# Expert weights of a mixture-of-experts stage fetched one expert per transfer, in runs of 8 KB

## The chip, the cores and the metric

The kernel runs on 1 core of one Trainium2 chip. The metric is the device time of one execution in microseconds (us); lower is better. The time before is 997.18 us, the median of 3 runs (996.82 to 998.98). Below, TensorE is PE, VectorE DVE, ScalarE ACT, GpSimd POOL, and SyncE, which issues the loads, SP.

## What is computed

One decoder block on 528 tokens (16 meta tokens and 512 real ones) of width 1024, in float32: two token mixers, then a mixture of experts, then a norm. The change touches the experts alone. Each token goes to 2 of 32 experts. An expert is two matrices of 1024 x 512 and one of 512 x 1024:

```
y = (silu(xb @ w_gate[e]) * (xb @ w_up[e])) @ w_down[e]
out = zeros.at[slot_tok].add(y * weight)
```

## The kernel before

The token mixers fill the first half of the time. Their weights, too, come in through SP (tiles `raw`), and between these SP already issues the first expert weights. Then the router picks experts (lines 885 to 960), and the loop `for p in range(last_p + 1)` runs over 16 pairs of experts. Each expert has room for 64 tokens, so a pair fills the 128 partitions of a result: expert 0 of the pair (`e` = 0) makes the partitions 0 to 63, expert 1 the others. In each pair:

- `ahead` (matmuls `pw`, line 976) finds the tokens of the next pair, and POOL gathers their rows from DRAM into `XG` (line 983);
- `up_proj` makes the gate product `pgt` and the up product `put` (line 1014): 8 steps over `k`, in each one matmul of expert 0 and one of expert 1;
- `glu` joins them on ACT and DVE into `HG`; `hidden_T` transposes it (`pht`); `operand` transposes the next pair's tokens (`pxs`, line 1006);
- `down_proj` (`py`, line 1033) has 4 steps over `k` for each of two halves of the columns, again with both experts in each;
- `combine` (`pcb`, line 1047) adds the previous pair's result to the tokens, 16 matmuls a pair.

Matmuls of the experts are float32 and fill half of the array's columns ("128*64" in the profile), those of `pcb`, `pw`, `pht` and `pxs` the whole array ("128*128"). The trace has two records for each float32 matmul instruction, one for `pcb` and the transposes. So the 16 instructions of one `put` are 32 records.

The weights of a pair come in 12 transfers of 1 MB, 4 for each of `w_gate`, `w_up` and `w_down`. `CUTS` says how they are cut. `fetch` (line 759) issues a transfer and notes in `at` which tile holds which part; `prefetch` issues as many as there are free buffers ("slots"); `take` hands a pair's tiles to the matmuls, `weight` picks one matmul's part, and `feed` gives the slots back after a product. Two places are cut otherwise and stay so: part of the first pair's gate (`pieces0`) and the last pair's `w_down`, in transfers of 512 KB. A loop behind the main one (line 1206) takes experts with more than 64 tokens; it is not entered with these inputs.

The order of `pgt`, `put`, `py`, `pw` and `pcb` on PE is not that of the text. A scheduler fixes each engine's order when the program is built, by its own estimate of when operands are there, so that a matmul whose weights it expects late goes behind others.

Of the kernel before, what the change touches and what calls it, by code (L numbers as in the profile page):

```python
# [8 lines left out]
F32 = mybir.dt.float32  # L9
# [29 lines left out]
def hybrid_block_kernel(ctx: ExitStack, tc: tile.TileContext, x, meta, norm1_g, w_in, hg_lb,  # L39
# [4 lines left out]
    PE, ACT, DVE, POOL, SP = nc.tensor, nc.scalar, nc.vector, nc.gpsimd, nc.sync  # L44
# [21 lines left out]
    def uniq(name):  # L66
        seq[0] += 1
        return f"{name}_{seq[0]}"

    def slot(shape, dtype, name):  # L70
        s = free.pop(0)
        return pool_of[s].tile(shape, dtype, name=uniq(name), tag=s), s

    def give(*ss):
        free.extend(ss)

    def ms(tag, shape, dtype, name):
        return misc.tile(shape, dtype, name=uniq(name), tag="m" + tag)

    def ps(shape, name, dtype=F32):  # L80
        return psum.tile(shape, dtype, name=name, tag="ps")

    def bc_row(ap1d, n):
        return bass.AP(tensor=ap1d.tensor, offset=ap1d.offset, ap=[[0, 128], [1, n]])
# [158 lines left out]
    for i in range(2):  # L243
        a, s = slot([128, 4, N], F32R, "hnH")
        b, s2 = slot([128, 4, N], F32R, "hnL")
# [13 lines left out]
    for i in range(5):  # L259
        t_ = tmp.tile([128, D], F32, name="xt", bufs=5)  # L260
# [72 lines left out]
    p = ps([128, 512], "pc")  # L333
# [74 lines left out]
    oaH, s = slot([128, 4, T], F32R, "oaH")  # L408
# [320 lines left out]
    for i in range(2):  # L729
        t_, s = slot([128, 2, D], F32, "h")  # L730
# [3 lines left out]
    def tk(lst, t, a=0, b=D):  # L734
        return lst[t // 2][:, t % 2, a:b]
# [2 lines left out]

    EW = [(w[0].rearrange("e (p k) c -> p e k c", p=128), nk) for w, nk in ((w_gate, 8), (w_up, 8), (w_down, 4))]
    last_p = NE // 2 - 1
    CUTS = [[(k, k + 2, 0, 512) for k in range(0, 8, 2)]] * 2 + [[(k, k + 1, 0, 1024) for k in range(4)]]
    pieces, pieces0 = [], []
    for p_ in range(last_p + 1):
        for m in range(3):
            cuts = CUTS[m]
            if p_ == 0 and m == 0:
                cuts = cuts[:2]
                pieces0 = [(0, 0, k, k + 1, 0, 512) for k in range(4, 8)]  # L750
            if p_ == last_p and m == 2:
                cuts = [(k, k + 1, c, c + 512) for c in (0, 512) for k in range(4)]
            pieces += [(m, p_) + c for c in cuts]
    at = {}
    nxt = [0]

    def fetch(t_, s, piece):
        m, p, k0, k1, c0, c1 = piece
        SP.dma_start(t_, EW[m][0][:, 2 * p:2 * p + 2, k0:k1, c0:c1])
        for k in range(k0, k1):  # L760
            at.setdefault((m, p), {})[k, c0 // 512] = (t_[:, :, k - k0], c0, s)

    def prefetch(n=len(pieces)):
        while n and nxt[0] < len(pieces) and free:
            n -= 1
            piece = pieces[nxt[0]]
            nxt[0] += 1
            t_, s = slot([128, 2, piece[3] - piece[2], piece[5] - piece[4]], F32, "wx")
            fetch(t_, s, piece)

    def weight(tab, e, k, c0):

        t_, b, _ = tab.get((k, c0 // 512)) or tab[k, 0]
        return t_[:, e, c0 - b:c0 - b + 512]

    def take(m, p):
        tab = at.pop((m, p))
        return tab, sorted({s for _, _, s in tab.values() if s})

    def gate(dst):  # L780
        got = []
# [213 lines left out]
    def token_onehots(i, sw):  # L995
        oht = OHT[:, i]
        DVE.tensor_scalar(oht, iotat, sw[:, 2:3], None, op0=OP.is_equal)
        return oht

    def operand():  # L1000

        xv = XG.rearrange("s (p k) -> s k p", k=8)
        for q in range(2):
            p_ = ps([128, 4, 128], "pxs")
            for k in range(4):
                PE.transpose(p_[:, k], xv[:, 4 * q + k], ident)  # L1006
            DVE.tensor_tensor(XS[:, 4 * q:4 * q + 4], p_,
                              g2k[:, 4 * q:4 * q + 4][:, :, None].to_broadcast([128, 4, 128]), op=OP.mult)

    def up_proj(w2, name):  # L1010
        p_ = ps([128, FE], name)
        for k in range(8):
            for e in range(2):
                PE.matmul(p_[CAP * e:CAP * e + CAP], XS[:, k, CAP * e:CAP * e + CAP],  # L1014
                          weight(w2, e, k, 0), start=(k == 0), stop=(k == 7))
        return p_

    def glu(pg, pu, sw):
        ACT.activation(HG, pg, AF.Silu, scale=sw[:, 1:2])  # L1019
        DVE.scalar_tensor_tensor(HG, pu, sw[:, 1:2], HG, op0=OP.mult, op1=OP.mult)  # L1020

    def hidden_T():

        pt = ps([128, 4, 128], "pht")
        hv = HG.rearrange("s (p k) -> s k p", k=4)
        for k in range(4):
            PE.transpose(pt[:, k], hv[:, k], ident)  # L1027
        ACT.activation(HT, pt.rearrange("p f s -> p (f s)"), AF.Copy)  # L1028
# [7 lines left out]
    def down_proj(w2, half, sw):  # L1036
        p_ = ps([128, 512], "py")
        down_steps(p_, w2, half, range(4))
        yh = Y[half][:, 0]
        ACT.activation(yh, p_, AF.Copy, scale=sw[:, 0:1])  # L1040
        DVE.scalar_tensor_tensor(Y[half][:, 1], p_, sw[:, 0:1], yh.bitcast(F32), op0=OP.mult, op1=OP.subtract)  # L1041

    def combine(oht, half):
        for t in range(4):
            p_ = ps([128, 512], "pcb")
            for i in range(2):
                PE.matmul(p_, oht[:, 128 * t:128 * t + 128], Y[half][:, i],  # L1047
                          start=(i == 0), stop=(i == 1))
            hs = tk(h32, t, 512 * half, 512 * half + 512)
            DVE.tensor_add(hs, hs, p_)  # L1050

    def ahead(p):

        onehots(OH, RK[:, :, 2 * p:2 * p + 2])
        pw = by_slot(OH, TAB[:, :, p])
        gather(pw[:, 3:4])
        return slot_weights(pw)
# [109 lines left out]


    wd, ss_ = take(2, last_p)
    u0, s = slot([128, 4, 512], F32, "u0")  # L1170
    sq, s2 = slot([128, 512], F32, "sqf")
# [29 lines left out]
    with tc.If(nr > 0):  # L1201
        XG = ms("A", [128, D], F32, "XG")
        POOL.memset(XG, 0.0)
        DVE.tensor_scalar(RK, RK, float(-CAP), None, op0=OP.add)
        with tc.For_i(0, nr):
            with tc.For_i(0, NE // 4) as i4:

                for i in range(2):
                    sw = ahead(i)
                    oht = token_onehots(i, sw)  # L1210
                    operand()
                    tabs, ss = [], []
                    for (w, nk), cuts in zip(EW, CUTS):
                        tabs.append({})
                        for k0, k1, _, c1 in cuts:
                            t_, s = slot([128, 2, k1 - k0, c1], F32, "wx")
                            SP.dma_start(t_, w[:, bass.ds(i4 * 4 + 2 * i, 2), k0:k1, :])
                            ss.append(s)
                            for k in range(k0, k1):
                                tabs[-1][k, 0] = (t_[:, :, k - k0], 0, s)  # L1220
                    glu(up_proj(tabs[0], "pgt"), up_proj(tabs[1], "put"), sw)
                    hidden_T()
                    for half in range(2):
                        down_proj(tabs[2], half, sw)
                        combine(oht, half)
                    give(*ss)
                rk2 = HG[:, :4 * NE].rearrange("p (t e) -> p t e", t=4)
                tab2 = HT[:, :8 * NE].rearrange("p (t e c) -> p t e c", t=4, c=4)
                DVE.tensor_copy(rk2[:, :, :NE - 4], RK[:, :, 4:])
                DVE.tensor_scalar(rk2[:, :, NE - 4:], RK[:, :, :4], float(-CAP), None, op0=OP.add)  # L1230
                DVE.tensor_copy(RK, rk2)
                DVE.tensor_copy(tab2[:, :, :NE // 2 - 2], TAB[:, :, 2:])
                DVE.tensor_copy(tab2[:, :, NE // 2 - 2:], TAB[:, :, :2])
                DVE.tensor_copy(TAB, tab2)

        gfb = ms("A", [128, D], F32, "gfb")
        SP.dma_start(gfb, bc_row(final_g, D))
        for t in range(4):
            sq, s = slot([128, D], F32, "sqf")
            o, s2 = slot([128, D], F32, "o")  # L1240
            ACT.activation(sq, tk(h32, t), AF.Square, accum_out=SS[:, 0, t:t + 1])
            rs = SS[:, 2, t:t + 1]
            rms_scale(rs, SS[:, 0, t:t + 1], D)
            DVE.scalar_tensor_tensor(o, tk(h32, t), rs, gfb, op0=OP.mult, op1=OP.mult)
            SP.dma_start(out2[128 * t:128 * t + 128], o)
            give(s, s2)
# [29 lines left out]
```

## Time and profile before

| what | value |
|---|---|
| median of 3 runs | 997.18 us (996.82 to 998.98) |
| the profiled execution: time, span | 998.75 us, 997.0 us |
| PE busy | 936.4 us (94%) |
| PE weight loads busy | 602.8 us (60%) |
| DVE, ACT, POOL busy | 448.3, 255.9, 246.0 us |
| read from DRAM, written | 250.89 MB, 4.19 MB |
| mean granted clock of PE | 0.974 |

The span runs from the first to the last instruction of the profiled execution, and times in the trace count from its start. Busy time of PE counts a matmul from its start to its modelled end, so a pipelined stream shows as fully busy. The profile's second part cuts the span into 40 slices of 24.9 us; PEclk there is the clock granted to PE in tenths of 2.4 GHz (9 stands for 90% or more), DMA the mean busy share of the core's 16 DMA engines, GB/s what they moved. In the timeline a row is a run of like instructions: start, length, engine, line, operation, result and operands, number of records.

### The profile page before, as it was taken

To read this page: it belongs to the slowest core of one execution; us is meant where nothing else is said; L and a number is where in the kernel's file an instruction comes from. 1 tells how busy PE (TensorE), PEld (TensorE's weight loads), DVE (VectorE), ACT (ScalarE), POOL (GpSimd) and SP (SyncE) were. 2 spreads that over 40 slices of the span, in tenths; PEclk is the share of its full clock that TensorE was granted. 3 is DMA by queue.
4 is the path that set the end of the run, shared out by engine and by line. 5 is a ranking of instruction groups with operands and counts; after the bars stand their busy time and mean duration, and the time that the engine had idled before them with its cause. 6 is when DMAs were issued, how large, how long until landed. Compare 5 with 4: busy or idle time off the path is not lost.

```text
span 997.0 us, 12289 instructions
## 1 busy us (share of the span) xinstructions
PE 936.4 (94%) x4812; PEld 602.8 (60%) x4812; DVE 448.3 (45%) x931; ACT 255.9 (26%) x456; POOL 246.0 (25%) x167
## 2 busy tenths in 40 slices
PE   7989999989979999999859999999999999999984
PEld 5979998879868888888733444443334343433331
DVE  5678448786772323232532443333334333333323
ACT  6445536876750000000401110100110100010004
POOL 4542443254465454545200000000000000000002
PEclk9999999999988999999959999999999999999998
DMA  6221112212563223238969999999999999999992
GB/s 215 77 92 45 44 53 85 62 45 85 218 236 100 96 91 99 92 99 312 389 258 328 409 407 408 408 409 408 409 409 409 408 408 408 408 408 409 409 356 87
DMA packets 94298, 251.76 MB, mean 253 GB/s; under 512 B 6582, under 2 KB 39434, under 8 KB 94235
## 3 DMA queue, kind: packets, MB, share of 16 engines
q1 hardware_dynamic: 91352, 244.61, 64.4%
q0 software_dynamic: 2304, 4.20, 1.2%
q10 hardware_dynamic: 578, 2.10, 0.5%
q8 instruction: 40, 0.66, 0.3%
q14 instruction: 24, 0.19, 0.1%
HBM read 250.89 MB, written 4.19 MB: 256 GB/s over the span
## 4 chain that ended last, share of the span: by engine, by line
PE 80%; DVE 7%; DMA 5%; ACT 4%; POOL 2%; issue 2%; SPq 0%; POOLq 0%; DVEq 0%; ACTq 0%
PE pj L204 27%; PE put L1014 11%; PE pgt L1014 10%; PE py L1033 10%; PE pcb L1047 7%; DMA wx<-in_w_up_dram 4%; PE po L799 3%; PE pl L545 2%; PE pw L976 2%; PE pxs L1006 1%; PE po L1071 1%; PE pj L311 1%; PE pht L1027 1%; POOL hl L91 1%; DMA XG<-HD,idx 1%
## 5 line engine op out<-in xcount | busy, mean ns | idle before, releaser
L204 PE MATMUL pj<-hnH,hl 128*128 128x512 f32 (+1 forms) x960 | 252.9, 353 | 9.5 <-POOL hl L91 7.2
L91 POOL TENSOR_TENSOR hl<-raw,hl 128x1024 fp32r<-128x1024 f32 (+1 forms) x76 | 174.9, 2303 | 202.2 <-ACT hl L88 100.0
L204 PEld LDWEIGHTS pj<-hnH,hl 128*128 128x128 f32 x960 | 163.9, 192 | 33.5 <-POOL hl L91 8.5
L204 PE MATMUL pj<-hnL,hl 128*128 128x512 f32 (+1 forms) x480 | 149.8, 349 | 0.0
L1050 DVE TENSOR_TENSOR h<-h,pcb 128x512 f32<-128x512 f32 x124 | 77.6, 683 | 110.3 <-PE pcb L1047 110.3
L1014 PE MATMUL put<-wx,XS 128*64 128x512 f32 x512 | 121.1, 600 | 2.0 <-DMA wx<-in_w_up_dram 2.0
L1014 PE MATMUL pgt<-wx,XS 128*64 128x512 f32 x512 | 119.5, 607 | 1.5 <-DMA wx<-in_w_gate_dram 1.5
L983 POOL DMA_INDIRECT XG<-HD,idx x16 | 16.5, 1031 | 409.7 <-DVE sw L992 250.5
L1033 PE MATMUL py<-wx,HG 128*64 128x512 f32 x512 | 115.5, 603 | 0.7 <-ACT HG L1028 0.7
L204 PEld LDWEIGHTS pj<-hnL,hl 128*128 128x128 f32 x480 | 85.4, 192 | 10.3
L1014 PEld LDWEIGHTS pgt<-wx,XS 128*64 128x64 f32 x512 | 36.2, 139 | 70.4 <-issue 64.3
L1033 PEld LDWEIGHTS py<-wx,HG 128*64 128x64 f32 x512 | 35.6, 138 | 67.5 <-issue 62.7
L1014 PEld LDWEIGHTS put<-wx,XS 128*64 128x64 f32 x512 | 33.6, 136 | 65.7 <-issue 61.8
L1047 PE MATMUL pcb<-Y,OHT 128*128 128x512 f32 x248 | 68.0, 411 | 0.0
L1047 PEld LDWEIGHTS pcb<-Y,OHT 128*128 128x128 f32 x248 | 43.5, 188 | 39.4 <-issue 30.8
L1041 DVE SCALAR_TENSOR_TENSOR Y<-py,sw,Y 128x512 fp32r<-128x512 f32 x31 | 23.3, 751 | 93.3 <-ACT Y L1040 92.3
L90 DVE CAST hl<-raw 128x1024 fp32r<-128x1024 f32 (+1 forms) x40 | 33.0, 824 | 63.5 <-PE pj L204 61.5
L1028 ACT ACTIVATE HG<-pht 128x512 f32<-128x512 f32 x16 | 9.6, 598 | 181.0 <-PE pht L1027 180.8
L1040 ACT ACTIVATE Y<-py,sw 128x512 fp32r<-128x512 f32 x31 | 21.3, 688 | 104.2 <-PE py L1033 104.2
L204 PE MATMUL pj<-obH,hl 128*128 128x512 f32 x128 | 40.7, 394 | 0.0
L1019 ACT ACTIVATE HG<-pgt,sw 128x512 f32<-128x512 f32 x16 | 11.0, 688 | 106.8 <-PE pgt L1014 106.8
L88 ACT ACTIVATE hl<-raw 128x1024 fp32r<-128x1024 f32 (+1 forms) x36 | 36.1, 1004 | 5.8 <-PE pj L311 3.1
(260 smaller groups left out, 1107.6 us busy)
## 6 DMA issues: line engine op xcount, KB each, us to landing
wx<-in_w_up_dram SPq DMA_DIRECT2D x64, 1024.0 KB, 18.3
wx<-in_w_gate_dram SPq DMA_DIRECT2D x62, 1024.0 KB, 18.4
wx<-in_w_down_dram SPq DMA_DIRECT2D x60, 1024.0 KB, 19.0
raw<-in_w_in_dram SPq DMA_DIRECT2D x24, 1024.0 KB, 5.1
raw<-in_w_up_b_dram SPq DMA_DIRECT2D x4, 1024.0 KB
raw<-in_w_out_dram SPq DMA_DIRECT2D x4, 1024.0 KB
wx<-in_w_down_dram SPq DMA_DIRECT2D x8, 512.0 KB, 17.2
h<-in_x_dram SPq DMA_DIRECT2D x2, 1024.0 KB
```

The costliest lines, as they stand in the source:

```text
L88: ACT.activation(hi, src, AF.Copy)
L90: he.tensor_copy(hi, src)
L91: le.tensor_sub(lo, src, hi.bitcast(F32))
L204: PE.matmul(o[:, :c1 - c0], w[:, k, :], hsl(a, k, c0, c1), start=(k == 0 and w is wh and a is aH), stop=(k == nk - 1 and w is wl))
L545: PE.matmul(pl[:, li % 2, c], zc, halves(zc, m)[1], start=True, stop=True)
L799: PE.matmul(p_, mg[:, a, k, 128 * t:128 * t + 128], w[:, k, :], start=(k == 0 and a == 0 and w is wh), stop=(k == 1 and a == 1))
L1014: PE.matmul(p_[CAP * e:CAP * e + CAP], XS[:, k, CAP * e:CAP * e + CAP], weight(w2, e, k, 0), start=(k == 0), stop=(k == 7))
L1033: PE.matmul(p_[CAP * e:CAP * e + CAP], HT[:, 128 * k + CAP * e:128 * k + CAP * e + CAP], weight(w2, e, k, 512 * half), start=(k == 0), sto ...
L1040: ACT.activation(yh, p_, AF.Copy, scale=sw[:, 0:1])
L1041: DVE.scalar_tensor_tensor(Y[half][:, 1], p_, sw[:, 0:1], yh.bitcast(F32), op0=OP.mult, op1=OP.subtract)
L1047: PE.matmul(p_, oht[:, 128 * t:128 * t + 128], Y[half][:, i], start=(i == 0), stop=(i == 1))
L1050: DVE.tensor_add(hs, hs, p_)
```

## The change

A transfer still has 1 MB, but in place of some rows `k` of both experts of a pair it holds twice as many rows of one expert. In DRAM the rows that one partition reads are neighbours within an expert, so each partition now reads one run of 8 KB where it read two of 4 KB. `note` records for each expert, row and half of the columns where it lies. The number of transfers, their size and the number of matmuls stay.

```diff
-    CUTS = [[(k, k + 2, 0, 512) for k in range(0, 8, 2)]] * 2 + [[(k, k + 1, 0, 1024) for k in range(4)]]
+    CUTS = [[(e, e + 1, k, k + 4, 0, 512) for k in (0, 4) for e in (0, 1)]] * 2 + \
+        [[(e, e + 1, k, k + 2, 0, 1024) for k in (0, 2) for e in (0, 1)]]
...
-                pieces0 = [(0, 0, k, k + 1, 0, 512) for k in range(4, 8)]
+                pieces0 = [(0, 0, 0, 2, k, k + 1, 0, 512) for k in range(4, 8)]
...
-                cuts = [(k, k + 1, c, c + 512) for c in (0, 512) for k in range(4)]
+                cuts = [(0, 2, k, k + 1, c, c + 512) for c in (0, 512) for k in range(4)]
...
+    def note(tab, t_, s, cut):
+        e0, e1, k0, k1, c0, c1 = cut
+        for e in range(e0, e1):
+            for k in range(k0, k1):
+                for c in range(c0, c1, 512):
+                    tab[e, k, c] = (t_[:, e - e0, k - k0, c - c0:c - c0 + 512], s)
...
     def fetch(t_, s, piece):
-        m, p, k0, k1, c0, c1 = piece
-        SP.dma_start(t_, EW[m][0][:, 2 * p:2 * p + 2, k0:k1, c0:c1])
-        for k in range(k0, k1):
-            at.setdefault((m, p), {})[k, c0 // 512] = (t_[:, :, k - k0], c0, s)
+        m, p, e0, e1, k0, k1, c0, c1 = piece
+        SP.dma_start(t_, EW[m][0][:, 2 * p + e0:2 * p + e1, k0:k1, c0:c1])
+        note(at.setdefault((m, p), {}), t_, s, piece[2:])
...
     def weight(tab, e, k, c0):
 
-        t_, b, _ = tab.get((k, c0 // 512)) or tab[k, 0]
-        return t_[:, e, c0 - b:c0 - b + 512]
+        return tab[e, k, c0][0]
```

The change also moves instructions on PE, since the scheduler counts with other transfers. In pairs 0 to 4 the order of the groups stays; in the 11 pairs 5 to 15 it becomes another, the same in all of them but for small things in the first and the last. The following shows pair 6. Its up weights are the tiles wx_4964, wx_5040, wx_5042 and wx_5044, its gate weights wx_4919, wx_4958, wx_4960 and wx_4962, and wx_4917 is the last of the pair ahead's down weights. In the changed kernel the first and third of four tiles are expert 0, the second and fourth expert 1.

PE in pair 6, from the end of the down product to the up product and `combine`, before (x4 is both experts at two `k`):

```order
L1033 MATMUL py<-wx_4917,HG_4334 64x512 x4
L1014 MATMUL pgt<-wx_4919,XS_4256 64x512 x4
L976 MATMUL pw<-TAB,OHI_4039 128x4 x4
L1014 MATMUL pgt<-wx_4958,XS_4256 64x512 x4
L1014 MATMUL pgt<-wx_4960,XS_4256 64x512 x4
L1014 MATMUL pgt<-wx_4962,XS_4256 64x512 x4
L1014 MATMUL put<-wx_4964,XS_4256 64x512 x4
L1047 MATMUL pcb<-Y_4332,OHT_4331 128x512 x7
L1014 MATMUL put<-wx_5040,XS_4256 64x512 x4
L1047 MATMUL pcb<-Y_4332,OHT_4331 128x512
L1047 MATMUL pcb<-Y_4333,OHT_4331 128x512 x5
L1014 MATMUL put<-wx_5042,XS_4256 64x512 x4
```

Each stretch of expert matmuls between two others has as many of expert 0 as of expert 1. (Behind the last row follow `pcb` x3, `put` x4 and `pht`.)

The gate product of pair 6 in the changed kernel, around `pw`:

```order
L1022 MATMUL pgt<-wx_4919,XS_4256 64x512
L984 MATMUL pw<-TAB,OHI_4039 128x4 x4
L1022 MATMUL pgt<-wx_4958,XS_4256 64x512
L1022 MATMUL pgt<-wx_4919,XS_4256 64x512
L1022 MATMUL pgt<-wx_4958,XS_4256 64x512
```

One matmul of expert 0 stands ahead of `pw` where there were four of both; the other 15 of `pgt` follow it, and then one `put` of expert 0.

The up product of pair 6 in the changed kernel, behind that one `put`:

```order
L1055 MATMUL pcb<-Y_4332,OHT_4331 128x512 x8
L1055 MATMUL pcb<-Y_4333,OHT_4331 128x512 x3
L1022 MATMUL put<-wx_5040,XS_4256 64x512
L1022 MATMUL put<-wx_4964,XS_4256 64x512
L1022 MATMUL put<-wx_5040,XS_4256 64x512
L1022 MATMUL put<-wx_4964,XS_4256 64x512
L1022 MATMUL put<-wx_5040,XS_4256 64x512
L1022 MATMUL put<-wx_4964,XS_4256 64x512
L1022 MATMUL put<-wx_5040,XS_4256 64x512
L1055 MATMUL pcb<-Y_4333,OHT_4331 128x512 x2
L1022 MATMUL put<-wx_5042,XS_4256 64x512
L1055 MATMUL pcb<-Y_4333,OHT_4331 128x512 x3
```

Then come 7 more of `put`, 4 of expert 1 and 3 of expert 0, and `pht`. `pcb` still cuts in three times, now in lots of 11, 2 and 3, and what it leaves between are stretches of 7, 1 and 7.

The first half of the down product of pair 6 in the changed kernel (wx_5046 is expert 0, wx_5065 expert 1; before, `py` took x4 of each tile, both experts in turn):

```order
L1041 MATMUL py<-wx_5046,HG_4334 64x512 x2
L1041 MATMUL py<-wx_5065,HG_4334 64x512
L1041 MATMUL py<-wx_5046,HG_4334 64x512
L1041 MATMUL py<-wx_5065,HG_4334 64x512 x2
L1041 MATMUL py<-wx_5046,HG_4334 64x512
L1041 MATMUL py<-wx_5065,HG_4334 64x512
```

The numbers of both experts are equal over these 8, but an expert's matmuls come two in a row. On SP the order of the transfers stays, with another shape in each row.

## Rows read from the trace of the kernel before

**Rows 1.** The page, the 40 slices: granted clock, and GB/s.
```profile
PEclk9999999999988999999959999999999999999998
GB/s 215 77 92 45 44 53 85 62 45 85 218 236 100 96 91 99 92 99 312 389 258 328 409 407 408 408 409 408 409 409 409 408 408 408 408 408 409 409 356 87
```
**Rows 2.** Stretches of pairs 2, 7, 14, 15: start:end length, busy PE, PEld, DVE, ACT, POOL (records), clock, DMA share, GB/s.
```profile
561.72:588.90 27.18, 27.18 (x134) 12.16 (x133) 10.15 (x24) 2.66 (x4) 0.99 (x1) 1.00 1.03 408
701.90:731.11 29.21, 28.29 (x133) 11.64 (x133) 10.49 (x24) 2.66 (x4) 1.03 (x1) 1.00 1.03 409
906.39:937.69 31.30, 28.73 (x133) 11.57 (x132) 9.60 (x20) 2.66 (x4) 0.99 (x1) 1.00 1.02 408
937.69:969.35 31.66, 29.06 (x133) 11.54 (x132) 8.25 (x13) 3.85 (x6) 0.00 (x0) 1.00 1.01 392
```
**Rows 3.** Waits of PE, 900 to 970 us: engine, tile, line <- awaited: total us, times, longest.
```profile
PE put L1014 <- DMA wx<-in_w_up_dram: 2.0, 2, 1.4
...
PE pgt L1014 <- DMA wx<-in_w_gate_dram: 1.5, 3, 0.7
```
**Rows 4.** Timeline of PE, one down product to the next.
```profile
701.90 7.09 PE L1033 MATMUL py<-wx,HG 128*64 128x512 f32 x32
708.82 1.89 PE L1014 MATMUL pgt<-wx,XS 128*64 128x512 f32 x8
710.63 1.05 PE L976 MATMUL pw<-TAB,OHI 128*128 128x4 f32 x8
711.62 5.37 PE L1014 MATMUL pgt<-wx,XS 128*64 128x512 f32 x24
716.82 1.89 PE L1014 MATMUL put<-wx,XS 128*64 128x512 f32 x8
718.63 1.89 PE L1047 MATMUL pcb<-Y,OHT 128*128 128x512 f32 x7
720.45 1.94 PE L1014 MATMUL put<-wx,XS 128*64 128x512 f32 x8
722.32 1.66 PE L1047 MATMUL pcb<-Y,OHT 128*128 128x512 f32 x6
723.91 1.94 PE L1014 MATMUL put<-wx,XS 128*64 128x512 f32 x8
725.78 0.97 PE L1047 MATMUL pcb<-Y,OHT 128*128 128x512 f32 x3
726.68 1.94 PE L1014 MATMUL put<-wx,XS 128*64 128x512 f32 x8
...
731.11 1.08 PE L1033 MATMUL py<-wx,HG 128*64 128x512 f32 x4
```
**Rows 5.** Timeline of PE's weight loads within that down product (in brackets the idle time ahead).
```profile
703.67 0.14 PEld L1033 LDWEIGHTS py<-wx,HG 128*64 128x64 f32 x2 [0.29 <-issue]
704.10 0.14 PEld L1033 LDWEIGHTS py<-wx,HG 128*64 128x64 f32 x2 [0.29 <-issue]
```
**Rows 6.** Timeline of PE, pair 0, behind its `pw`.
```profile
523.77 0.64 PE L1014 MATMUL put<-wx,XS 128*64 128x512 f32 x1
523.78 0.64 PE L1014 MATMUL pgt<-wx,XS 128*64 128x512 f32 x1
524.25 0.59 PE L1014 MATMUL put<-wx,XS 128*64 128x512 f32 x1
```
**Rows 7.** Timeline of PE, the last `combine`: float32 on the whole array.
```profile
981.63 3.70 PE L1187 MATMUL pcb<-HG,OHT 128*128 128x512 f32 x8 [0.85 <-DVE HG L1184]
```
**Rows 8.** Stretches as in rows 2: the last transfers' runs of 2 KB, then runs of 4 KB.
```profile
962.00:965.00 3.00, 3.00 (x17) 1.54 (x15) 1.29 (x2) 0.00 (x0) 0.00 (x0) 1.00 1.04 384
...
800.00:900.00 100.00, 97.23 (x451) 39.90 (x449) 35.81 (x78) 8.67 (x13) 4.12 (x4) 1.00 1.03 409
```
**Rows 9.** The page, DMA issues: transfers, KB of each, us to landing.
```profile
wx<-in_w_up_dram SPq DMA_DIRECT2D x64, 1024.0 KB, 18.3
```
**Rows 10.** The chain that ended last, at the start of pair 0: start, us, what.
```profile
503.28 7.22 DMA XG<-HD,idx
```

More of the change, by code (lines that the diff above doesn't have):

```diff
@@ L767, in prefetch @@
             nxt[0] += 1
-            t_, s = slot([128, 2, piece[3] - piece[2], piece[5] - piece[4]], F32, "wx")
+            e0, e1, k0, k1, c0, c1 = piece[2:]
+            t_, s = slot([128, e1 - e0, k1 - k0, c1 - c0], F32, "wx")
             fetch(t_, s, piece)
     def weight(tab, e, k, c0):
-        t_, b, _ = tab.get((k, c0 // 512)) or tab[k, 0]
-        return t_[:, e, c0 - b:c0 - b + 512]
+        return tab[e, k, c0][0]
     def take(m, p):
         tab = at.pop((m, p))
-        return tab, sorted({s for _, _, s in tab.values() if s})
+        return tab, sorted({s for _, s in tab.values() if s})
     def gate(dst):
@@ L1214, in hybrid_block_kernel @@
                         tabs.append({})
-                        for k0, k1, _, c1 in cuts:
-                            t_, s = slot([128, 2, k1 - k0, c1], F32, "wx")
-                            SP.dma_start(t_, w[:, bass.ds(i4 * 4 + 2 * i, 2), k0:k1, :])
+                        for cut in cuts:
+                            e0, e1, k0, k1, _, c1 = cut
+                            t_, s = slot([128, e1 - e0, k1 - k0, c1], F32, "wx")
+                            SP.dma_start(t_, w[:, bass.ds(i4 * 4 + 2 * i + e0, e1 - e0), k0:k1, :])
                             ss.append(s)
-                            for k in range(k0, k1):
-                                tabs[-1][k, 0] = (t_[:, :, k - k0], 0, s)
+                            note(tabs[-1], t_, s, cut)
                     glu(up_proj(tabs[0], "pgt"), up_proj(tabs[1], "put"), sw)
```

## The prediction

> **What bounds the kernel now.** I read the 40 slices first [rows 1]. From slice 22 on (about 550 us) the loads run at 408 GB/s to the end, and nothing in the program moves bytes faster: DMA is full in the whole expert stage. That invites the thought that a faster load shortens the stage in proportion. The second view speaks against it. I cut the stage at the starts of the down products, one pair of experts each [rows 2]. Pair 2 takes 27.18 us, pair 7 takes 29.21 and pairs 14 and 15 take 31.30 and 31.66, at the same load rate and at full clock. If loads set the pace, all would be alike. They are not, since loads run ahead of use: a transfer lands 18.3 us after its issue [rows 9]. PE eats up a stock of loaded weights, and PE's own order sets the length of a pair until the stock is gone. The waits of PE between 900 and 970 us show where it is: here, in pairs 14 and 15, PE stands waiting for up and gate weights [rows 3].
>
> How much do these waits cost? A pair in the order of pairs 7 to 13 takes 29.21 us, so pair 14 lost 31.30 - 29.21 = 2.1 us. Pair 15 has other work in it; I put its loss at 2.6, from 31.66 - 29.21 = 2.45 and a bit for the `pw` that it lacks. Together **4.7 us: all that faster loads can give back** as long as PE's order stays.
>
> **PE's beat.** Within a down product two weight loads come every 0.43 us [rows 5], one for each half of the array's columns, and 32 records take 6.9 to 7.1 us [rows 4]: two records run at once, 0.43 us each, one for expert 0 and one for expert 1. An instruction is two records, so a matmul of both experts takes one slot of 0.86 us, for two instructions. Does a single expert's matmul take half a slot, or a whole one? The last `combine` is float32 on the whole array, nothing beside it, and has 8 records in 3.70 us [rows 7], 0.46 each with the start: a record takes 0.43 us alone, too. So **a matmul without a partner costs the whole 0.86 us**. Can the halves run apart? In pair 0 the order is put of expert 0, then gate of experts 0 and 1, then put of expert 1. The trace has put and gate start at 523.77 and 523.78 [rows 6]: the gate of expert 1 did not wait for that of expert 0. Each half works down its own list, so what counts in a stretch is the longer list, not strict alternation.
>
> A stretch ends where `pw`, `pcb` or a transpose uses the whole array: [rows 4] have put x8 from 720.45 to 722.32, 1.87 us for 2 slots (1.72), then `pcb`, then put again, and no expert matmul starts before the `pcb` is through. A half that has run out can't take work from behind it.
>
> **The change part by part.** Transfers, their size, and SP's order stay, so SP pays nothing. Slots are freed a little later: a tile of four `k` is done after 3.4 us of a product, one of two `k` after 1.7. The 18.3 us of issued transfers [rows 9] cover that; without them the loads would stand 1.7 us a product.
>
> *Loads.* No row shows a run of 8 KB. From 2 KB to 4 KB the rate went from 384 to 409 GB/s, 6% [rows 8]; from 4 to 8 KB I bound it by nothing and the same again, and 6% less on the other side, because nothing here excludes a loss. I take 2%. With 4.7 us of waits to remove over the stage, this ends at -4.7 us at most.
>
> *PE's order.* I count slots from one down product to the next as the longer list of each stretch. Before, in pairs 5 to 15: down product and first gates 10, rest of the gate and first put 8, then 2, 2, 2: 24. The rows agree: 8.73 us for the 10 (701.90 to 710.63) and 7.01 for the 8 (711.62 to 718.63) [rows 4]. Now: down product and one gate of expert 0: 9. Behind `pw`, 15 gates (8 of expert 1, 7 of expert 0) and a put of expert 0, which fills the hole: 8. Then `pcb` cuts in, and the remaining puts come in lots of 7, 1 and 7, of which the longer lists are 4, 1 and 4. Sum 9 + 8 + 4 + 1 + 4 = 26. **Two slots more, 1.72 us, in each of 11 pairs: 18.9 us.** The cuts themselves are as many as before (`pw`, three of `pcb`, the transposes), so their switching costs nothing more. The doubled order in `py` has equal lists and I cost it at nothing; the cover is that each half runs its own list [rows 6].
>
> *Together.* A pair grows from 29.2 to 30.9 us. Loads took 31.3 us a pair where PE waited for them [rows 2], and the stock lasted 9 pairs at 29.2, so it was worth 9 x 2.1 = 19 us. At 30.9 it shrinks by 0.4 a pair or not at all: the waits of pairs 14 and 15 go, whatever the new load rate is between -4% and any gain. So the sum is +18.9 - 4.7 = **+14.2 us**.
>
> *At the start* the first gather takes 7.22 us on the chain [rows 10]. Each of its rows may get behind a packet with 4 KB more; for 8 rows on each of 16 engines at 408/16 = 25.5 GB/s that is 8 x 0.16 = 1.3 us as an upper end, an estimate; lower end nothing, which I take, for the transfers issued just ahead of it are those that keep their 2 KB runs.
>
> The profiled execution took 998.75 us, with a span of 997.0; the sum makes it 1012.95. The median of the runs shown lies 1.57 lower, at 997.18, so I predict **1011.4 us**.
>
> *A rule against it.* Weight loads of 0.14 us start while matmuls run back to back, so they are hidden [rows 4, 5]. The Trainium skill (TensorE: Matmul & The Clock Gate, Part 3, The mechanism) says that a weight load overlaps running matmuls only when its row group differs; both experts use all rows here, so by that rule no load would be hidden. Here the trace disagrees. But a matmul alone in its half may be another matter: with its two loads of 0.14 in the open, 22 slots would cost 6.2 us more, 1017.6; I keep that for the range.
>
> **The rivals.**
> 1. *Lone matmuls cost nothing, and loads get faster* (**faster**): should a half without a partner run its records in half the time, a pair stays at 29.2 us and the loads are the limit. At 1% more rate (4.7 us in the 430 us of full load) the waits are gone: 997.2 - 4.7 = 992.5. For it: the rate rose from 2 to 4 KB. Against: the 0.46 us of a lone float32 record [rows 7]. Chance 0.07. The Trainium skill (DMA: Bandwidth & Descriptors, Why small descriptors are slow) gives each packet a fixed cost of about 3 cycles in the engine beside one cycle per 32 bytes: 3 on 128 for 4 KB, so 1.2% less for 8 KB, an estimate that would just do for this rival. No run here shows it yet.
> 2. *Nothing happens*: 8 KB runs are cut into 4 KB again, and lone matmuls cost nothing: 997. Against: needs both. Chance 0.04. (The first alone leaves my forecast as it is.)
> 3. *The doubled down order stalls*: if a second matmul of the same half holds up the other half, each `py` loses up to 2 slots, 10 pairs x 1.72 = 17 more: 1029. Against: [rows 6]. Chance 0.05.
> 4. *8 KB runs are slower*: loads become the limit from 30.9 + 19/10 = 32.8 us a pair, 5% below today's rate. At 6%, over 430 us, loads end 27 us later: 1024. Chance 0.04.
>
> **How the numbers follow.** Forecast 0.80, rivals 0.07, 0.04, 0.05, 0.04. About 0.2% is what a measurement of this kernel can tell from no change. Slower: 0.80 + 0.05 + 0.04 = 0.89; same 0.04; faster 0.07. The range: below, if one of the two lone slots in a pair were covered after all, 11 x 0.86 = 9.5 less, 1002; above, the open weight loads and the gather, +6.2 + 1.3, about 1019, and one more for rounding: 1002 to 1020. It leaves all rivals out.
>
> **What would show it.** Right: pairs 6 to 13 take 30.9 us from down product to down product, up from 29.2; PE has no wait on `wx` late in the stage; weight loads of `put` appear singly with 0.43 us between; GB/s falls or pauses at times, for slots are full. The pairs 1 to 4 stay at 27.2. Wrong: pairs at 29.2 or below (rivals 1, 2), a down product longer than 7.1 us (rival 3), or waits on `wx` in the middle of the stage (rival 4).

## Result, and the profile after the change

The changed kernel took 1010.08 us (median, 1009.59 to 1011.09), the kernel before on the same chip 997.29 us (996.82 to 998.98): a ratio of 1.0126, interval 1.0109 to 1.0144. The change makes the kernel **1.3% slower**. 1011.4 had been forecast, with a range of 1002 to 1020.

The profiled execution took 1011.09 us, its span was 1009.4, so 12.4 us were added to the 997.0 of before. The page first, the same lines as [rows 1], and the count of packets, of which 94,235 of 94,298 were under 8 KB before:

```profile
PEclk9999999999989999999879999999999999999998
GB/s 213 85 84 43 43 53 88 92 21 84 229 223 97 84 103 88 101 90 409 390 181 395 421 420 419 420 419 421 420 420 419 420 421 421 420 420 421 386 4 87
DMA packets 70489, 251.76 MB, mean 249 GB/s; under 512 B 6581, under 2 KB 39433, under 8 KB 46618
```

The transfers do what the diff says: 23,871 packets are now of 8 KB or more (63 before), and the loads run at 420 GB/s in place of 408. DMA got **3% faster and the kernel got slower**: it did not run at the pace of its loads. The slice of 4 GB/s, the last but one, shows the loads through early, with PE still at work (the 87 of the last slice stood there before, too). Next the stretches, columns as in [rows 2]: pairs 2, 7, 14, 15, again cut at the down products.

```profile
561.63:588.79 27.16, 27.16 (x135) 12.14 (x136) 10.11 (x24) 2.66 (x4) 0.99 (x1) 1.00 1.01 420
705.12:736.01 30.89, 29.98 (x135) 12.71 (x136) 10.39 (x24) 2.66 (x4) 1.02 (x1) 1.00 1.01 421
921.32:952.19 30.87, 29.96 (x134) 12.70 (x136) 9.58 (x20) 2.66 (x4) 0.99 (x1) 1.00 1.01 412
952.19:983.54 31.35, 30.11 (x132) 13.58 (x132) 8.18 (x13) 3.85 (x6) 0.00 (x0) 1.00 0.20 74
```

Pair 2 is as before, pair 7 takes 30.89 us where it took 29.21, pair 14 takes 30.87 where it took 31.30. The clock stands at 1.00 in all of them, and PE is busy 1.7 us longer in pair 7 (29.98 against 28.29) with as many records (135 and 133): the pair is longer because of how the records stand, not for a wait or the clock. The waits of PE from 540 to 985 us, in the columns of [rows 3], are two, and none is for `wx`:

```profile
PE pht L1035 <- DVE HG L1028: 9.6, 11, 0.9
PE py L1041 <- ACT HG L1036: 0.7, 1, 0.7
```

So the 3.5 us of waits for weights in [rows 3] are gone. Where the time went is in PE's timeline of pair 7, which answers to [rows 4]:

```profile
705.05 7.14 PE L1041 MATMUL py<-wx,HG 128*64 128x512 f32 x32
711.97 1.02 PE L1022 MATMUL pgt<-wx,XS 128*64 128x512 f32 x2
712.92 1.05 PE L984 MATMUL pw<-TAB,OHI 128*128 128x4 f32 x8
713.91 6.65 PE L1022 MATMUL pgt<-wx,XS 128*64 128x512 f32 x29
...
720.92 2.81 PE L1055 MATMUL pcb<-Y,OHT 128*128 128x512 f32 x11
723.67 3.65 PE L1022 MATMUL put<-wx,XS 128*64 128x512 f32 x14
727.24 0.73 PE L1055 MATMUL pcb<-Y,OHT 128*128 128x512 f32 x2
727.91 1.07 PE L1022 MATMUL put<-wx,XS 128*64 128x512 f32 x2
728.91 0.96 PE L1055 MATMUL pcb<-Y,OHT 128*128 128x512 f32 x3
729.80 3.65 PE L1022 MATMUL put<-wx,XS 128*64 128x512 f32 x14
734.37 0.75 PE L1035 MATMUL pht<-ident,HG 128*128 128x128 f32 x4 [0.92 <-DVE HG L1028]
```

Read the counts against the times; a matmul is two records. `put` x2, one matmul, takes 1.07 us; an x4, one matmul of each expert, takes 1.08 (the last row shown in this section). `put` x14 is seven matmuls and takes 3.65 us; eight (x16) take 3.65 as well, as the first experiment shows below. Where a list is odd, its last matmul has no partner and still takes its slot. The weight loads of that `put` x14, in the columns of [rows 5], show the end of the list: two loads every 0.43 us while both halves work, then one:

```profile
725.43 0.14 PEld L1022 LDWEIGHTS put<-wx,XS 128*64 128x64 f32 x2 [0.28 <-issue]
725.87 0.14 PEld L1022 LDWEIGHTS put<-wx,XS 128*64 128x64 f32 x1 [0.29 <-issue]
726.29 0.14 PEld L1022 LDWEIGHTS put<-wx,XS 128*64 128x64 f32 x1 [0.29 <-issue]
```

Two small steps more. The first gather on the chain answers to [rows 10], 0.24 us longer than its 7.22:

```profile
502.93 7.46 DMA XG<-HD,idx
```

And the end of the program differs in the clock. From the last pair's down product to the end of the span it is 997.0 - 969.36 = 27.64 us before and 1009.4 - 983.54 = 25.86 after. In the kernel before, some 3 us of it stood at half the clock, the lower level of 1.2 GHz, as a stretch in the columns of [rows 2] and the last down product in the timeline show:

```profile
971.00:973.00 2.00, 2.00 (x6) 0.49 (x4) 0.00 (x0) 0.00 (x0) 0.00 (x0) 0.50 0.04 14
```
```profile
969.36 6.21 PE L1033 MATMUL py<-wx,HG 128*64 128x512 f32 x20 [0.75 <-ACT HG L1028]
```

The same 20 records of the changed kernel, at full clock, take 1.70 us less (the second row is the x4 spoken of above, a little later in the same product):

```profile
983.54 4.51 PE L1041 MATMUL py<-wx,HG 128*64 128x512 f32 x20 [0.75 <-ACT HG L1036]
...
988.41 1.08 PE L1041 MATMUL py<-wx,HG 128*64 128x512 f32 x4
```

The sum by the timelines, from the starts of the down products of pairs 4 and 15: 643.05 - 643.23 = -0.18 us up to pair 4; then (983.54 - 643.05) - (969.36 - 643.23) = 340.49 - 326.13 = **+14.36** in pairs 5 to 15; then 25.86 - 27.64 = -1.78 at the end. Together +12.4.

### The profile page after: what moved, and what is told of

Same layout as the page of the kernel before. It is cut to its first block, busy times and chain, and to the rows that moved or that the text cites. A ratio compares the mean times of both kernels' runs of the same rounds, so it can differ in the third digit from the quotient of the medians.

```text
span 1009.4 us, 12289 instructions
## 1 busy us (share of the span) xinstructions
PE 952.4 (94%) x4812; PEld 615.0 (61%) x4812; DVE 447.3 (44%) x931; ACT 255.8 (25%) x456; POOL 245.5 (24%) x167
## 4 chain that ended last, share of the span: by engine, by line
PE 79%; DVE 8%; ACT 6%; POOL 2%; issue 2%; DMA 1%; POOLq 0%; SPq 0%; DVEq 0%; ACTq 0%
PE pj L204 23%; PE pgt L1022 12%; PE put L1022 12%; PE py L1041 11%; PE pcb L1055 6%; PE po L807 3%; PE pw L984 2%; PE pxs L1014 2%; PE pl L545 1%; PE po L1079 1%; PE pj L311 1%; PE pht L1035 1%; POOL hl L91 1%; DVE HG L1028 1%; ACT hl L88 1%
## 5 line engine op out<-in xcount | busy, mean ns | idle before, releaser
L1022 PE MATMUL put<-wx,XS 128*64 128x512 f32 x512 | 139.6, 598 | 0.0
L1022 PE MATMUL pgt<-wx,XS 128*64 128x512 f32 x512 | 127.3, 606 | 0.0
L1022 PEld LDWEIGHTS pgt<-wx,XS 128*64 128x64 f32 x512 | 39.8, 139 | 72.5 <-issue 72.2
L1022 PEld LDWEIGHTS put<-wx,XS 128*64 128x64 f32 x512 | 39.5, 136 | 70.1 <-issue 69.9
L1041 PEld LDWEIGHTS py<-wx,HG 128*64 128x64 f32 x512 | 40.5, 136 | 61.3 <-issue 58.2
L1028 DVE SCALAR_TENSOR_TENSOR HG<-put,sw,HG 128x512 f32<-128x512 f32 x16 | 12.0, 750 | 58.8 <-PE put L1022 52.5
```

The costliest lines, as they stand in the source:

```text
L1041: PE.matmul(p_[CAP * e:CAP * e + CAP], HT[:, 128 * k + CAP * e:128 * k + CAP * e + CAP], weight(w2, e, k, 512 * half), start=(k == 0), sto ...
```

## Experiments

My theory: the time is in lone matmuls of PE's order, nothing of it in the transfers. The rivals: that the 8 KB runs or the tiles of one expert cost the time by themselves; that the doubled sequence of the down product does; that the swapped sequence of experts matters by itself. The medians, and the ratio to the kernel before on the same chip:

| kernel | median us | ratio, interval |
|---|---|---|
| change, expert 1 first | 989.17 | 0.9917, 0.9904 to 0.9930 |
| before, expert 1 first | 997.90 | 1.0001, 0.9992 to 1.0009 |
| change for w_down alone | 994.24 | 0.9965, 0.9953 to 0.9977 |
| change with runs of 4 KB | 1010.84 | 1.0131, 1.0116 to 1.0146 |
| change for gate and up alone | 1011.51 | 1.0137, 1.0119 to 1.0155 |
| change, expert 1 first, lone put | 987.83 | one run |

**Another order, the same transfers.** The change with this edit, in `up_proj` and in `down_steps`:

```diff
-            for e in range(2):
+            for e in (1, 0):
```

> The change, with the two experts in the other sequence in every gate, up and down product (expert 1 ahead of expert 0); transfers as in the change, the sums the same. The scheduler then writes an order without lone matmuls: 24 slots of 0.86 us from one down product to the next in place of 26. Theory (lone matmuls cost whole slots, loads at 420 GB/s are then the limit): PE alone would need about 27.7 to 29.2 us a pair, the loads 12.85 MB / 420 GB/s = 30.6 us; the stage runs off its stock and then waits for loads near its end, which come some 12 us earlier than before; 985 to 993 us, under both kernels. Rival (longer runs or single-expert tiles themselves cost the time, the order nothing): stays at about 1010. Rival (the order matters, but 8 KB gives no rate): about 997.

989.17 us: as the theory says, and faster than either kernel. The transfers are those of the change, 420 GB/s. PE's timeline of one pair:

```profile
754.46 7.09 PE L1041 MATMUL py<-wx,HG 128*64 128x512 f32 x32
761.37 3.60 PE L1022 MATMUL pgt<-wx,XS 128*64 128x512 f32 x16
764.91 1.05 PE L984 MATMUL pw<-TAB,OHI 128*128 128x4 f32 x8
765.89 3.65 PE L1022 MATMUL pgt<-wx,XS 128*64 128x512 f32 x16
769.38 3.60 PE L1022 MATMUL put<-wx,XS 128*64 128x512 f32 x16
772.91 3.24 PE L1055 MATMUL pcb<-Y,OHT 128*128 128x512 f32 x13
776.08 3.65 PE L1022 MATMUL put<-wx,XS 128*64 128x512 f32 x16
779.67 0.97 PE L1055 MATMUL pcb<-Y,OHT 128*128 128x512 f32 x3
780.66 0.75 PE L1035 MATMUL pht<-ident,HG 128*128 128x128 f32 x4
```

All counts of the experts' products are 16 or 32, no list is odd: 24 slots. The pair takes 782.23 - 754.46 = 27.77 us, 3.1 less than in the change and 1.4 less than before with its 24 slots. Two slots are 1.72. The rest is this order's own gain: `pcb` x3 stands between the last `put` and the transposes, so the wait of `pht` for VectorE, 0.92 us in each pair of the change and of before, is covered; and `put` and `pcb` come in fewer lots, which leaves some 0.5 us.

Now the loads are the limit in the last pairs. The windows of pairs 13 and 14, and the waits of PE from 860 to 962 us, which take in pair 15 as well:

```profile
866.50:897.00 30.50, 28.28 (x133) 12.32 (x132) 10.29 (x24) 2.66 (x4) 1.04 (x1) 1.00 1.01 420
897.00:927.97 30.97, 28.30 (x134) 12.34 (x133) 9.41 (x20) 2.66 (x4) 0.99 (x1) 1.00 1.01 420
```
```profile
PE put L1022 <- DMA wx<-in_w_up_dram: 3.9, 3, 1.3
PE pgt L1022 <- DMA wx<-in_w_gate_dram: 3.4, 4, 1.3
```

A pair needs 12 transfers of 1024 KB, 12.58 MB, and its share of the 4.20 MB of gathers, 0.26 MB: 12.84 MB at 420 GB/s is 30.6 us, about what the two rows show. Here the faster loads pay. The last pair's down product starts at 960.35, 9.0 us before that of the kernel before, where I had put the lead of the loads at some 12; 0.6 of the 9.0 goes again at the end, where this trace has a longer stretch at half the clock.

**The same swap on the kernel before**, as a control.

> Control: the kernel before, with the same swap of the two experts in every product and its own transfers of two runs of 4 KB. The groups of PE's order and its 24 slots a pair stay as before. Theory: 997 us within 0.2%, loads at 408 GB/s, waits on wx in the last pairs as before. Rival (the swap itself is what gains or loses time, by the half of the array that starts first): the same step against before that the swapped change shows against the change.

997.90 us, no change: pairs 6 to 12 still take 29.21 us, and PE still waits for weights in pairs 13 to 15, 4.7 us by its rows:

```profile
PE put L1014 <- DMA wx<-in_w_up_dram: 3.1, 3, 1.6
PE pgt L1014 <- DMA wx<-in_w_gate_dram: 1.6, 3, 0.6
```

The sequence of the two experts is worth nothing in itself. It gained above because, with tiles of one expert, it decides in which order PE's instructions are laid out.

**Half of the change: w_down alone.** Gate and up get their old cut back:

```diff
-    CUTS = [[(e, e + 1, k, k + 4, 0, 512) for k in (0, 4) for e in (0, 1)]] * 2 + \
+    CUTS = [[(0, 2, k, k + 2, 0, 512) for k in range(0, 8, 2)]] * 2 + \
```

> Only w_down in transfers of one expert with runs of 8 KB, gate and up as before. PE's order has 24 slots a pair, and the doubled sequence of experts in the down product that the change has. Theory (lone gate and up matmuls are the cost): the loads reach about 412 GB/s, most of the 4.7 us of waits on wx goes, pairs stay at 29.2 us: about 993. Rival (the doubled down order or the tiles of one expert cost the time): 1005 or more. Rival (nothing but the order of gate and up counts and the rate gives nothing): 997.

994.24 us, close to the 993 of the theory. One pair with its load rate, what is left of the waits, and the doubled down product:

```profile
701.80:731.10 29.30, 28.37 (x135) 12.42 (x136) 10.53 (x24) 2.66 (x4) 1.03 (x1) 1.00 1.02 413
```
```profile
PE put L1022 <- DMA wx<-in_w_up_dram: 0.4, 1, 0.4
```
```profile
701.76 7.14 PE L1041 MATMUL py<-wx,HG 128*64 128x512 f32 x32
```

With PE at 24 slots, a third of the weights in 8 KB runs lifts the rate to 413 GB/s, and of the 3.5 us of waits in [rows 3] 0.4 are left. The last down product starts at 965.71, 3.65 us earlier. The doubled sequence costs 7.14 - 7.09 = 0.05 us a product. That it would stall is out.

**The change with two runs of 4 KB in each transfer.** A tile of gate or up holds rows 0, 1, 4, 5 or 2, 3, 6, 7 in place of four in a row, one of `w_down` rows 0, 2 or 1, 3 (all pairs but pair 0, which keeps its runs of 8 KB):

```diff
+            src = EW[m][0][:, 2 * p + e0].rearrange("p (a b i) c -> p b a i c", a=2, b=2)[:, b]
+            SP.dma_start(t_.rearrange("p e (a i) c -> p (e a) i c", a=2), src)
...
-        for k in range(8):
+        for k in order8[0]:
```

> The change with its transfers of one expert each, but two runs of 4 KB a partition in each: a tile of gate or up holds k 0, 1, 4, 5 or 2, 3, 6, 7, one of w_down k 0, 2 or 1, 3, and the products take their k in that sequence, so PE's order is that of the change with its 26 slots (the sums over k are added up in another sequence). Theory (the time is in PE's order, the run length is nearly idle): the loads at 408 GB/s as before, 31.5 us a pair against 30.9 of PE, so the stock still lasts: 1010 us, within 3. Rival (runs of 8 KB cost the time in some way, in the array of engines or in the tiles): back to about 997.

1010.84 us, where the change took 1010.08. The rate is back at 408 to 409 and the pairs stay long:

```profile
705.30:736.20 30.90, 29.99 (x135) 12.71 (x135) 10.41 (x24) 2.66 (x4) 1.03 (x1) 1.00 1.03 409
```

PE has no wait for `wx` here either: at 30.9 us a pair even loads of 31.4 us (12.84 MB at 409) last to the end from the stock. So in the changed kernel the **run length is worth nothing**, neither gain nor loss; the loss comes with the tiles of one expert, by way of PE's order.

**The other half: gate and up alone.** w_down gets its old cut back:

```diff
-        [[(e, e + 1, k, k + 2, 0, 1024) for k in (0, 2) for e in (0, 1)]]
+        [[(0, 2, k, k + 1, 0, 1024) for k in range(4)]]
```

> Only gate and up in transfers of one expert with runs of 8 KB, w_down in transfers of both experts with two runs of 4 KB as before: the other half of the change. PE's order has the 26 slots a pair of the change. Theory (the lone matmuls of gate and up are the whole cost): pairs of 30.9 us, no wait on wx, loads between 412 and 420 GB/s by the share of 8 KB runs and full slots at times: 1010 us within 2. Rival (the transfers of w_down carry part of the cost): 1003 or less.

1011.51 us, pairs of 30.88, no wait for `wx`, 414 to 419 GB/s. The lone `put` stands between two lots of `pcb` as in the change:

```profile
727.88 1.07 PE L1022 MATMUL put<-wx,XS 128*64 128x512 f32 x2
```

The whole loss is in gate and up; the transfers of w_down had no part in it. With the run of w_down alone this splits the change in two: one half gains 0.35% by its loads, the other loses 1.4% by its order, and with both the loads' gain is not seen.

**A lone list, measured by itself.** From the swapped change, expert 0's up product is cut down:

```diff
+                if e or k == 0 or name == "pgt":
```

> The swapped change (expert 1 first) with expert 0's up product left out but for its k 0 (7 of its 8 matmuls in every pair are not computed); all weights are still loaded. So put is, but for one matmul, a list of expert 1 alone: stretches of 4 matmuls in one half of the columns, the other half empty. Theory (a matmul without a partner costs a whole slot): such a stretch takes the 3.6 us that 8 matmuls of both experts took (4 x 0.86 and the start), weight loads 0.86 us apart two by two, and a pair stays at 27.4 to 28 us while the stock lasts. Rival (a half without a partner goes at twice the pace): 1.9 us a stretch and pairs of about 24.4 us. The time as a whole tells little, since the loads set the end in both cases: 984 to 989 us.

The records decide, not the time of 987.83 us. PE's timeline of one pair, from its up product:

```profile
772.67 3.60 PE L1023 MATMUL put<-wx,XS 128*64 128x512 f32 x10
776.20 3.97 PE L1056 MATMUL pcb<-Y,OHT 128*128 128x512 f32 x16
780.10 3.65 PE L1023 MATMUL put<-wx,XS 128*64 128x512 f32 x8
784.67 0.75 PE L1036 MATMUL pht<-ident,HG 128*128 128x128 f32 x4 [0.92 <-DVE HG L1029]
```

`put` x10 and x8 take 3.60 and 3.65 us, exactly what two lots of `put` x16 took in the swapped change. **Nearly half of the records are gone (18 for 32) and no time was saved.** Their weight loads:

```profile
780.59 0.14 PEld L1023 LDWEIGHTS put<-wx,XS 128*64 128x64 f32 x1 [0.29 <-issue]
781.01 0.14 PEld L1023 LDWEIGHTS put<-wx,XS 128*64 128x64 f32 x1 [0.29 <-issue]
```

One load every 0.43 us, as in a full pace; I had written "0.86 us apart two by two" of them, which was wrong, since each of a matmul's two records has its own load. The pair takes 786.25 - 757.75 = 28.50 us, half a microsecond over what I expected, for `put` again stands right ahead of the transposes and the wait of 0.92 us is back.

## Why the prediction was right, step by step

- *What bounds the kernel.* Right: not the loads, but PE's order until the stock is gone. 3% more rate bought nothing, and with the rate taken back the time stayed within 0.08%.
- *Two slots more a pair.* 1.72 us were counted. Pairs 6 to 13 took 30.88 in place of 29.21: 1.67, and pairs 5 to 14 together (952.12 - 643.05) - (937.70 - 643.23 - 2.1) = 16.7, with pair 14's wait taken off. That a matmul without a partner costs a whole slot was argued from a lone `combine` [rows 7]; the run with the lone list shows it.
- *The waits.* All of them went, as said, and 4.7 us was near what they were worth. Pair 14's 2.1 was right. Pair 15's 2.6 can be held against the run with `w_down` alone, where PE has the groups of that pair in the order of before: 965.71 - 935.84 = 29.87 us, with 0.44 of one wait left in it. Less that wait, and 0.05 for the doubled down order, it is 29.38; so about 31.66 - 29.38 = 2.28 us of pair 15 were waits, and together with pair 14 it is 4.4. It may be 0.2 more, if the wait that is left also cost its stretch a new start (an x4 takes 1.08 us for a slot of 0.86).
- *Pair 15.* By the same 29.38 the order cost this pair more than two slots: after the change, with no wait for weights, it takes 983.54 - 952.12 = 31.42, which is 2.04 more. Before, ten records of `pgf`, work for the norm that only the last pair has, stood between the last `put` and the transposes (first row below); after, two do, and `pht` stands 0.50 us for VectorE (second row). The prediction named the `pw` that pair 15 lacks, and not `pgf`. So the order cost 16.7 + 2.04 = 18.7 where the sum had 18.9: two slots were a little too dear in ten pairs, and the wait in pair 15 was left out. That these nearly cancel is luck. In all, 18.74 - 4.38 = 14.36 as measured, 14.2 predicted. How much of it goes to the order and how much to the waits rests on the 29.38; the difference does not.

```profile
966.55 1.38 PE L1147 MATMUL pgf<-gf,ident 8*128 8x128 f32 x10
982.05 0.75 PE L1035 MATMUL pht<-ident,HG 128*128 128x128 f32 x4 [0.50 <-DVE HG L1028]
```

- *The end of the program.* This term wasn't in the sum: in the profiled execution before, half the clock cost the last down product 1.7 us, and that of the change ran at full clock. That is why the profiled execution took 1011.09 and not 1012.95. Between the medians the step is 12.8 us; both medians lie under their profiled executions, and where these runs saved it no trace tells.
- *Load rate.* Taken at +2%, measured +3% (408 to 420). The range held it, and since no wait was left the size changed nothing. The Trainium skill (DMA: Bandwidth & Descriptors, Why small descriptors are slow) gave an estimate of 1.2%; the measured gain is over twice that. Not right was that GB/s would fall or pause: 30.6 us of loads a pair against 30.9 of PE are nearly in balance, and the rate held at 420 until the last transfers were out.
- *Costed at nothing.* The first gather grew by 0.24 us of the 1.3 allowed. The doubled down order costs 0.05 us a product, so rival 3 is out. Weight loads of lone matmuls stay hidden: 0.14 us inside each 0.43, so the 6.2 us kept for the range do not exist. The Trainium skill (TensorE: Matmul & The Clock Gate, Part 3, The mechanism) says that weight loads overlap running matmuls only where the row group differs, though a paragraph ahead of that it also lets those into the background weight buffer go ahead; the trace disagrees with the "only" for lone matmuls, too.
- *The rivals.* Rival 1 needed free lone matmuls, rival 2 as well; rival 4 needed slower loads. All three are shown false. Rival 1's other half was true: with an order of 24 slots the faster loads do pay, as the swapped kernel shows.

What stays argued: why the scheduler lays out the order as it does. That it takes the tile that the code loads second as the later one fits the swap, but no run shows its reckoning.

## What to carry to other kernels

Where two matmuls share the array by halves of its columns, as here, count a stretch by the longer of its two lists, cut at each instruction that takes the whole array; an odd one costs as much as a pair. A change of transfer shape can move the order on PE, so read the new order before the gain in GB/s, and when it has gone bad, mend the order (here one loop's sequence) rather than drop the transfer: both together made 989 us out of 997. And a faster transfer is worth only the waits for it that a row shows.

## What the runs showed of the hardware

- Load rate by run length, same queue: 384 GB/s in the stretch of 2 KB [rows 8], 408 to 409 at 4 KB, 420 at 8 KB; with 8 KB for w_down alone 413, for gate and up alone 416. The step from 4 to 8 KB is half of that from 2 to 4 KB, and mixtures lie between.
- Each column half follows its own list even where the code's sequence does not alternate: the doubled down order, in which one expert has two matmuls in a row, takes 7.14 us against 7.09.
- While the last pair's down product ran, the clock stood at half for some us in three of the eight traces (before, w_down alone, and the swapped change) and not in the others, the control with its like waits among them. The swapped change paid most, in its last down product:

```profile
960.35 8.10 PE L1041 MATMUL py<-wx,HG 128*64 128x512 f32 x24 [0.75 <-ACT HG L1036]
```

From 958 to 960 us its granted clock was 0.76, with PE busy 1.60 of the 2 us, and from 960 to 964 it was 0.50. In the control PE was busy 1.47 and 1.79 of 2 us in the like place (969 to 971, 971 to 973), at 1.00. What made the difference these rows don't tell; 1.7 us and more of a run's end hang on it.
